# A mixer and mixture-of-experts layer on one core: pieces of 64 for heavy experts, earlier returns of weight buffers, and mask products of 128 rows

## The chip, the core and the metric

The kernel runs on one core of one Trainium2 chip. A core has four engines that compute: TensorE (PE in the profile, its weight loads PEld), VectorE (DVE), ScalarE (ACT) and GpSimd (POOL). SyncE (SP) issues DMAs; POOL and ACT can issue them too. Each engine works through its own instructions in order, and they wait for each other by semaphores. The metric is the time of one launch on the device in microseconds; lower is better.

## What is computed

One layer over 2048 tokens of width 1024. First a mixer: an RMS norm, one input projection, four heads of mLSTM and four heads of differential attention, an output projection and the residual. Then a mixture of experts, with these lines:

```python
h = rms_norm(x, norm1_w)
x = x + hybrid_mixer(h, ...)              # mLSTM heads and differential attention heads
h = rms_norm(x, norm2_w)
x = x + hierarchical_moe(h, ...)
...
# differential attention, per block of 128 queries
mask = key_chunk[None, :] <= q_chunk[:, None]          # chunks of 64 keys
p = softmax(where(mask, q @ k.T * scale, -inf))        # two maps per head
attn = p[:, :, 0] - lam * p[:, :, 1]
...
# experts: the best of 4 groups, then the best 2 of its 8 experts, for each token
weights = g_w * softmax(top_vals)
hid = silu(xb @ w_gate[e]) * (xb @ w_up[e])            # 1024 -> 512
y_expert = hid @ w_down[e]                             # 512 -> 1024
y = sum over the two experts of weights * y_expert
```

There are 32 experts and 4096 places for tokens (two for each token), 128 on average. With these inputs twelve experts get more than 128: six get 129 to 150, four get 165 to 189, two get 201 and 241.

## The kernel before

**Stages.** The input projection (to about 345 us), the heads in 64 steps (4 heads by 16 blocks of 128 queries, 345 to 1140 us), the output projection with the second norm and the choice of experts (to about 1405 us), then the experts. Weights are float32. Each is split into a high and a low part (`split_h` on ACT, line 66, `split_l` on DVE, line 70), and products are made three times (high by high, high by low, low by high).

**Mask.** In `score_atoms` two products per chunk of keys make the scores of a block (line 574). On the chunk with the diagonal, a third product (line 577) adds -1e30 where the first 64 queries meet the last 64 keys: `qm` and `km` are one row of 128 bf16 numbers each. There are 64 blocks with two maps each, so 128 such products.

**Slot tables.** `tb_d` holds for every expert a list of slots; a slot is a row of four numbers: the token to gather, half of its weight, the row to return to. Unused slots return to spare rows behind the output. `fetch_slots(i)` (line 1176) loads an expert's first 256 slots into a tile `ix2`; five such tiles exist, and the fetch for expert e+3 takes over the tile of expert e-2.

**One iteration per expert.** The first 128 slots go through TensorE with split weights: `ffn1` (line 1227, 48 products of 512 columns) for expert e, and then `ffn2` (line 1242, 24 products, called through `down(0)` to `down(3)`) for expert e-1. The result is evicted with the slot's weight (line 1247) and returned by an indirect DMA that adds into the output (`scatter`, line 1251). Every such return waits until the one before it has landed. `ready` issues the splits of the weights six halves ahead.

**Further slots.** An expert with more than 128 tokens (n > P) is heavy. Under branches on its count, `few` takes slots 129 to 160 (a piece of 32), then 161 to 192 (another piece of 32, if n > 160), then 193 to 256 (a piece of 64, if n > 192). A piece uses the raw weights in float32: its tokens are turned (line 1261), multiplied with gate and up (line 1272), turned again (line 1278) and multiplied with down (line 1287). The first piece has `down(2)` and `down(3)` of the expert before between its steps. Its result is evicted to `yE` (line 1304), scaled by the slots' weights on POOL (line 1305), and after all pieces `yE` is returned with 128 rows.

**Weights.** Twelve buffers of 1 MB hold raw weights, six for an expert. `done(e, j)` hands back buffer j of expert e, that is, SP issues the load of expert e+2 into it (lines 847 and 850, issue order on SP's queue). All six `done` of an iteration stand behind the branch: first the two `w_down` buffers of expert e-1, then the four gate and up buffers of expert e. Each DMA on SP's queue waits for the DMA eight places before it.

**Order of the experts.** A small computation on the chip ranks the experts: those over `HEAVY` = 144 tokens are spread evenly among the others, the j-th of them at (j + `LEAD`)/count. Two experts are fixed at the front. The iterations then run, with L for light, q for one piece, M for two pieces (32 + 32) and X for three: LLLLqLqqLLqLLLXLLXLLMLLLMLqMLLMq.

## Time and profile before

| | |
|---|---|
| median of 3 runs | 2278.22 us (2277.26 to 2286.74) |
| profiled execution, its own time | 2281.88 us |
| its span | 2279.8 us, 40566 instructions |
| busy: PE, PEld, DVE, ACT, POOL | 92%, 77%, 70%, 54%, 23% of the span |
| HBM over the span | 378.51 MB read, 87.65 MB written, 204 GB/s |

The span is the time from the first to the last instruction in the trace; the run's own time is 2.1 us more. The trace names each instruction by line, engine, operation and tiles, so `pgu<-H,xT` is a product that writes pgu from H and xT. Behind an instruction stand, in brackets, the idle time of its engine before it and what ended that. The DMA share is the mean busy share of the 16 DMA engines; it can pass 1 where packets overlap.

### The profile page before, as it was taken

To read this page: it belongs to the slowest core of one execution; us is meant where nothing else is said; L and a number is where in the kernel's file an instruction comes from. 1 tells how busy PE (TensorE), PEld (TensorE's weight loads), DVE (VectorE), ACT (ScalarE), POOL (GpSimd) and SP (SyncE) were. 2 spreads that over 40 slices of the span, in tenths; PEclk is the share of its full clock that TensorE was granted. 3 is DMA by queue.
4 is the path that set the end of the run, shared out by engine and by line. 5 is a ranking of instruction groups with operands and counts; after the bars stand their busy time and mean duration, and the time that the engine had idled before them with its cause. 6 is when DMAs were issued, how large, how long until landed. Compare 5 with 4: busy or idle time off the path is not lost. (4 is left out here: it accounts for less than half of the span.)

```text
span 2279.8 us, 40566 instructions
## 1 busy us (share of the span) xinstructions
PE 2099.1 (92%) x13815; PEld 1754.8 (77%) x13816; DVE 1603.2 (70%) x4373; ACT 1230.7 (54%) x2820; POOL 518.5 (23%) x684
## 2 busy tenths in 40 slices
PE   7999989999999999999999996998888999888885
PEld 6888878899999899999877884866666656665664
DVE  6667646886887687788877777876765747666562
ACT  4444324665566566566633334766665656655653
POOL 4000013223322332332111113222232222222312
PEclk9999998999999999999999997999999999999998
DMA  7656368636554663555169442999997859778783
GB/s 220 184 162 188 132 150 226 157 107 163 165 133 116 179 173 105 153 154 145 52 196 302 149 140 92 336 307 303 332 297 257 290 184 317 255 279 269 232 296 48
DMA packets 242336, 452.95 MB, mean 199 GB/s; under 512 B 36368, under 2 KB 120400, under 8 KB 232080
## 3 DMA queue, kind: packets, MB, share of 16 engines
q1 hardware_dynamic: 192160, 316.56, 41.8%
q0 software_dynamic: 49632, 131.86, 22.2%
q8 instruction: 153, 2.51, 0.5%
q10 hardware_dynamic: 272, 1.05, 0.1%
q14 instruction: 119, 0.97, 0.1%
HBM read 378.51 MB, written 87.65 MB: 204 GB/s over the span
## 5 line engine op out<-in xcount | busy, mean ns | idle before, releaser
L70 DVE TENSOR_TENSOR L<-R,H 128x1024 fp32r<-128x1024 f32 x408 | 485.4, 1221 | 184.8 <-ACT H L66 177.7
L66 ACT ACTIVATE H<-R 128x1024 fp32r<-128x1024 f32 x408 | 417.6, 1060 | 154.3 <-DMA R<-w_up 117.9
L1227 PE MATMUL pgu<-H,xT 128*128 128x512 f32 x1024 | 369.1, 418 | 49.7 <-DVE th L1209 28.7
L1227 PEld LDWEIGHTS pgu<-H,xT 128*128 128x128 f32 x1024 | 199.5, 195 | 98.5 <-ACT H L66 28.2
L589 ACT ACTIVATE prob<-sc,nm 128x512 f32<-128x512 f32 (+3 forms) x320 | 196.0, 625 | 51.0 <-DVE nm L586 45.8
L578 DVE TENSOR_REDUCE mx<-sc 128x1 f32<-128x512 f32 (+3 forms) x320 | 187.8, 605 | 35.5 <-PE sc L577 19.4
L1227 PE MATMUL pgu<-L,xT 128*128 128x512 f32 x512 | 207.6, 406 | 0.0
L574 PE MATMUL sc<-kt,qt 128*128 128x512 f32 (+3 forms) x640 | 192.7, 388 | 7.7 <-DMA kt<-k_d 7.2
L1242 PE MATMUL py<-H,hT 128*128 128x512 f32 x512 | 175.4, 405 | 2.1 <-ACT y L1247 1.1
L94 PE MATMUL w<-H,hs 128*128 128x256 f32 x512 | 156.8, 306 | 4.8 <-DVE num L694 4.8
L504 PE MATMUL w<-hs,H 128*128 128x256 f32 x512 | 159.2, 311 | 0.5 <-ACT tho L549 0.5
L633 PE MATMUL w<-va,aT 128*128 128x128 f32 x1088 | 156.3, 277 | 2.2 <-ACT raw L514 1.4
L478 POOL DMA_DIRECT2D qt<-q_d x128 | 78.1, 617 | 299.7 <-DVE g_lf L407 275.4
L633 PEld LDWEIGHTS w<-va,aT 128*128 128x128 f32 x1088 | 139.1, 191 | 8.6 <-ACT raw L514 4.1
L95 PE MATMUL w<-L,hs 128*128 128x256 f32 x512 | 145.8, 285 | 0.0
L96 PE MATMUL w<-H,hs 128*128 128x256 f32 x512 | 145.5, 284 | 0.0
L506 PE MATMUL w<-hs,L 128*128 128x256 f32 x512 | 145.4, 284 | 0.0
L505 PE MATMUL w<-hs,H 128*128 128x256 f32 x512 | 145.3, 284 | 0.0
L1242 PEld LDWEIGHTS py<-H,hT 128*128 128x128 f32 x512 | 97.5, 190 | 31.1 <-issue 7.2
L1251 POOL DMA_INDIRECT out<-y,ix x32 | 58.4, 1825 | 259.8 <-ACT y L1247 166.1
L1227 PEld LDWEIGHTS pgu<-L,xT 128*128 128x128 f32 x512 | 100.3, 196 | 19.8 <-issue 2.3
L1305 POOL TENSOR_SCALAR yE<-yE,ix 32x1024 f32<-32x1024 f32 (+1 forms) x20 | 57.0, 2848 | 253.0 <-ACT yE L1304 130.3
(373 smaller groups left out, 5283.6 us busy)
## 6 DMA issues: line engine op xcount, KB each, us to landing
R<-w_gate SPq DMA_DIRECT2D x128, 512.0 KB, 11.5
R<-w_up SPq DMA_DIRECT2D x128, 512.0 KB, 12.4
R<-w_down SPq DMA_DIRECT2D x63, 1024.0 KB, 8.2
hs<-hT_d POOLq DMA_DIRECT2D x62, 1024.0 KB, 5.4
hT_d<-hs SPq DMA_DIRECT2D x16, 1024.0 KB, 4.1
qt<-q_d POOLq DMA_DIRECT2D x128, 128.0 KB, 6.1
xt<-x SPq DMA_DIRECT2D x30, 512.0 KB, 4.4
q_d<-qkT SPq DMA_DIRECT2D x32, 256.0 KB, 3.7
```

The lines of the kernel that those rows point to most:

```text
L66: return A.activation(dst, src, AF.Copy, scale=scale)
L70: return V.tensor_tensor(dst, src, h.bitcast(F32), OP.subtract)
L94: T.matmul(ps, xh, wh, start=start, stop=False)
L95: T.matmul(ps, xh, wl, start=False, stop=False)
L96: T.matmul(ps, xl, wh, start=False, stop=stop)
L504: T.matmul(ps, l0, m0, start=d == 0, stop=False)
L574: T.matmul(ps[:, :n], QT[g // 2][:, o, m, g % 2 * P:(g % 2 + 1) * P], KT[r * 4 + c][:, m, :n], start=o == 0, stop=o == 1 and c < sb)
L578: V.reduce_max(B["mx"][:, m, c:c + 1], ps[:, :n], axis=AX.X)
L589: mark["ACT"] = A.activation(B["p", m][:, c2 * 512:c2 * 512 + n], B["sc", m, c2][:, :n], AF.Exp, bias=nm, scale=0.125, accum_out=B["rs"][: ...
L633: T.matmul(po, B["aT", c][:, kb * P:(kb + 1) * P], VA[r * 4 + c][:, kb, :], start=c == 0 and kb == 0, stop=c == nch - 1 and kb == nb[c] - 1)
L1227: T.matmul(pgu[c], xT[:, l, d, :], r[:, :, n], start=d == 0 and m == 0, stop=d == DC - 1 and m == 2)
L1242: T.matmul(py[n], hT[:, l, f, :], r[:, c], start=f == 0 and m == 0, stop=f == 3 and m == 2)
```

## The change

1. `qm` and `km` have 128 rows; all but the first are zero. The mask product runs over 128 rows and adds the same.
2. Further slots come as one piece of 32 (n up to 160) or one piece of 64 (n up to 192), and a second piece of 64 above. `few` is cut into `few_down`, `few_emit` and `few_return`.
3. The eviction of a piece takes the slot's weight as its scale. For that each table tile has three more columns of slots, laid out as the pieces lie in PSUM, and `fetch_slots` loads them with eight more small DMAs. The scaling on POOL is gone. Each piece is returned by itself, with 32 or 64 rows.
4. The `done` of the two `w_down` buffers are issued during `ffn1` (at d = 3 and 5). The `done` of the four gate and up buffers stand inside the two sides of the branch; on the light side they wait for the splits and not for the branch's end on PE.
5. `HEAVY` is 128 and `LEAD` 0.5. The order becomes LLLqLqLLqLqLLXLXLLMLqLLqLMLLMLML.
6. The tile of ones for the ranking is made later, in the pool of the output projection.

```diff
--- before.py
+++ after.py
@@ -41,8 +41,8 @@
 XAT = 1
 LOOK = 6
 PR = (0, 1, 2, 3, 4)
-LEAD = 0.7
-HEAVY = 144
+LEAD = 0.5
+HEAVY = 128
 NRM = 0.49
 QK1 = (0.0, 0.45)
 QK0 = (0.5, 0.95)
@@ -117,7 +117,6 @@
 
         ident = cp.tile([P, P], F32, name="ident")
         before = cp.tile([P, P], BF16, name="before")
-        onesb = cp.tile([P, P], BF16, name="onesb")
         nw = cp.tile([P, 2], F32, name="nw")
         cnt = cp.tile([P, NE], F32, name="cnt")
 
@@ -135,13 +134,13 @@
             V.tensor_scalar(ident, jp, 0.0, None, op0=OP.is_equal)
             V.tensor_scalar(before, jp, 0.0, None, op0=OP.is_gt)
             V.tensor_scalar(cmask, jp, 0.0, NEG, op0=OP.is_lt, op1=OP.mult)
-        V.memset(onesb, 1.0)
-        qm = c1.tile([1, P], BF16, name="qm")
+
+        qm = c1.tile([P, P], BF16, name="qm")
         V.memset(qm, 0.0)
-        V.memset(qm[:, 0:64], NEG)
-        km = c1.tile([1, P], BF16, name="km")
+        V.memset(qm[0:1, 0:64], NEG)
+        km = c1.tile([P, P], BF16, name="km")
         V.memset(km, 0.0)
-        V.memset(km[:, 64:128], 1.0)
+        V.memset(km[0:1, 64:128], 1.0)
         ones64 = c1.tile([64, P], F32, name="ones64")
         V.memset(ones64, 1.0)
 
@@ -939,6 +938,8 @@
             V.tensor_copy(m3[:, 2, :], ident[:NE, :NE])
             ones32 = sp.tile([NE, NE], F32, name="ones32", bufs=1)
             V.memset(ones32, 1.0)
+            onesb = sp.tile([P, P], BF16, name="onesb", bufs=1)
+            V.memset(onesb, 1.0)
             V.memset(cnt, 0.0)
             V.tensor_tensor(wr, wr, n2c.unsqueeze(2).to_broadcast([P, DC, NL]), OP.mult)
 
@@ -1180,9 +1181,13 @@
                     else:
                         eid[i] = nc.values_load(cnti[:1, ids_at + i:ids_at + i + 1], engines=(mybir.EngineType.SP, mybir.EngineType.Activation)[:2 if i < 3 else 1], min_val=0,
                                                 max_val=NE - 1, skip_runtime_bounds_check_because="a place's expert")
-                    IX[i] = sp.tile([P, 2, 4], F32, name="ix2", bufs=AHEAD + 2)
+
+                    IX[i] = sp.tile([P, 5, 4], F32, name="ix2", bufs=AHEAD + 2)
                     e = eid[i]
-                    nc.sync.dma_start(IX[i], tb_d[ds(e * SLOTS, 2 * P), :].rearrange("(k p) c -> p k c", p=P))
+                    nc.sync.dma_start(IX[i][:, :2], tb_d[ds(e * SLOTS, 2 * P), :].rearrange("(k p) c -> p k c", p=P))
+                    for k, m, r0 in ((2, Q, 0), (3, M, 0), (4, M, M)):
+                        for q in range(P // m):
+                            nc.sync.dma_start(IX[i][q * m:(q + 1) * m, k], tb_d[ds(e * SLOTS + P + r0, m), :])
 
             def gather(ix, xg):
 
@@ -1288,21 +1293,25 @@
                                  raw[:, q * w:(q + 1) * w], start=f == 0, stop=f == 3, skip_group_check=True)
                 return px
 
-            def few(e, m, r0, between=()):
+            def few_down(e, m, xH, between=()):
 
                 between = list(between) + [lambda: None] * 2
-                xH = few_turn_x(m, r0)
                 between[0]()
                 hH = sp.tile([P, 2, P], F32, name="hH", bufs=1)
                 th = [few_ffn1(xH, e, m, c) for c in range(m // Q)]
                 between[1]()
                 for c, t in enumerate(th):
                     few_turn_h(t, hH, c)
-                px = few_ffn2(hH, e, m)
-                w = D * m // P
+                return few_ffn2(hH, e, m)
+
+            def few_emit(e, m, r0, px):
+                w, k = D * m // P, 2 if m == Q else 3 + r0 // M
                 for q in range(P // m):
-                    A.activation(yE[r0:r0 + m, q * w:(q + 1) * w], px[q * m:(q + 1) * m, :w], AF.Copy)
-                G.tensor_scalar(yE[r0:r0 + m], yE[r0:r0 + m], IX[e][r0:r0 + m, 1, 1:2], None, op0=OP.mult)
+                    A.activation(yE[r0:r0 + m, q * w:(q + 1) * w], px[q * m:(q + 1) * m, :w], AF.Copy,
+                                 scale=IX[e][q * m:(q + 1) * m, k, 1:2])
+
+            def few_return(e, m, r0):
+                scatter(yE[r0:r0 + m], IX[e][:m, 4 if r0 else 1])
 
             engines = [mybir.EngineType.PE, mybir.EngineType.DVE, mybir.EngineType.Activation, mybir.EngineType.Pool]
             why = "counts of 2048 tokens"
@@ -1339,14 +1348,16 @@
                             turn(xTn, xg0, (d // 4,))
                             if d == 5 and e + 2 < NE:
                                 gather(IX[e + 2][:, 0], xg0)
+                        if d in (3, 5) and e:
+                            done(e - 1, 4 + d // 4)
                         if d == 4:
                             tc.mark_branch_hint_location(f"more{e}", n > P, engines)
                     thn = [hidden(p, 256) for p in pgu]
                 else:
+                    emit(*waiting)
                     hT = new_hT()
                     for d in range(2):
                         turn_h(th[d], hT, d)
-                    emit(*waiting)
                     thn = None
                 if e:
                     py = new_py()
@@ -1360,28 +1371,37 @@
                 down(0)
                 down(1)
                 if e < NE:
+                    last = (lambda: down(2), lambda: down(3))
                     with tc.If(n > P, label=f"more{e}", preferred_fallthrough_block=True) as more:
                         tc.mark_branch_hint_location(f"more{e}b", n > P + Q, engines)
-                        few(e, Q, 0, (lambda: down(2), lambda: down(3)))
-                        with tc.If(n > P + Q, label=f"more{e}b", preferred_fallthrough_block=True):
+                        with tc.If(n > P + Q, label=f"more{e}b", preferred_fallthrough_block=True) as many:
                             tc.mark_branch_hint_location(f"more{e}c", n > P + M, engines)
-                            few(e, Q, Q)
-                            with tc.If(n > P + M, label=f"more{e}c", preferred_fallthrough_block=True):
-                                few(e, M, M)
-                        scatter(yE, IX[e][:, 1])
+                            px = few_down(e, M, few_turn_x(M, 0), last)
+                            with tc.If(n > P + M, label=f"more{e}c", preferred_fallthrough_block=True) as most:
+                                xH = few_turn_x(M, M)
+                                few_emit(e, M, 0, px)
+                                few_return(e, M, 0)
+                                few_emit(e, M, M, few_down(e, M, xH))
+                                few_return(e, M, M)
+                            with most.Else():
+                                few_emit(e, M, 0, px)
+                                few_return(e, M, 0)
+                        with many.Else():
+                            few_emit(e, Q, 0, few_down(e, Q, few_turn_x(Q, 0), last))
+                            few_return(e, Q, 0)
+                        for j in range(4):
+                            done(e, j)
                     with more.Else():
-                        down(2)
-                        down(3)
+                        for f in last:
+                            f()
+                        for j in range(4):
+                            done(e, j)
                 else:
                     down(2)
                     down(3)
                 if e:
                     waiting = (py, IX[e - 1][:, 0])
-                    for j in (4, 5):
-                        done(e - 1, j)
                 if e < NE:
-                    for j in range(4):
-                        done(e, j)
                     xT, th = xTn, thn
             emit(*waiting)
             sched.__exit__(None, None, None)
```

On SP, the queue of loads, around the fetch of a later expert's table (`ix<-tb_d`) in one iteration. Before, from the fetch to the loads of `w_down`:

```order
L1185 DMA ix_18971<-tb_d 128x2x4 [waits DMASW2_49,DMASW1_49,DMASW4_49,DMASW0_49,DMAHW2_49,Activation_49,Pool_49]
L1325 TENSOR_LOAD cnti
L1363 COMPARE_AND_BRANCH
L1366 COMPARE_AND_BRANCH
L1369 COMPARE_AND_BRANCH
L1369 UNCONDITIONAL_BRANCH x2
L1366 UNCONDITIONAL_BRANCH
L1363 UNCONDITIONAL_BRANCH x2
L850 ISA
L850 DMA R_15378<-w_down 128x2x1024 [waits DMAHW3_49,DVE_49,PE_49]
L850 ISA
L850 DMA R_18092<-w_down 128x2x1024 [waits DMAHW4_49,DVE_49,PE_49]
```

After, the last four of the nine DMAs of a fetch, and what follows; the one of both halves (128x2x4) and four of 32 rows stand ahead of these rows:

```order
L1190 ISA
L1190 DMA ix_19043<-tb_d 64x4 [waits DMAHW7_49]
L1190 ISA
L1190 DMA ix_19043<-tb_d 64x4 [waits DMAHW0_49]
L1190 ISA
L1190 DMA ix_19043<-tb_d 64x4 [waits DMAHW1_49]
L1190 ISA
L1190 DMA ix_19043<-tb_d 64x4 [waits DMAHW2_49]
L1334 TENSOR_LOAD cnti
L849 ISA
L849 DMA R_15376<-w_down 128x2x1024 [waits DMAHW3_49,DVE_49,PE_49]
L849 ISA
```

The loads of `w_down` stand ahead of the branches now, and eight small DMAs stand ahead of them, each with a wait for an earlier DMA.

On PE, in the branch of a heavy expert. Before, the end of the first piece of 32 (`px<-R,hH`), the branch, and the second piece of 32 (`pt<-ident,xg` turns its tokens, `px<-R,xH` is gate and up):

```order
L1287 MATMUL px<-R_15378,hH 32x256 x8
L1287 MATMUL px<-R_18092,hH 32x256 x8
L1366 COMPARE_AND_BRANCH
L1367 REGISTER_ALU
L1434 BRANCH_PREFETCH_HINT
L1261 MATMUL pt<-ident,xg_18094 128x32 x8
L1272 MATMUL px<-R_15374,xH 32x256 x8
L1272 MATMUL px<-R_15375,xH 32x256 x8
L1272 MATMUL px<-R_15376,xH 32x256 x8
L1272 MATMUL px<-R_15377,xH 32x256 x8
L1278 MATMUL pt<-ident,th_18837 128x128
L1287 MATMUL px<-R_15378,hH 32x256 x8
```

After, behind the branch for more than 160 tokens, the piece of 64 is the first, and the products of the expert before (`py`) stand inside it:

```order
L1377 COMPARE_AND_BRANCH
L1378 REGISTER_ALU
L1454 BRANCH_PREFETCH_HINT
L1266 MATMUL pt<-ident,xg_18094 128x64 x8
L1247 MATMUL py_18704<-H_117,hT 128x512
L1247 MATMUL py_18704<-L_119,hT 128x512
L1247 MATMUL py_18704<-H_117,hT 128x512
L1247 MATMUL py_18705<-H_117,hT 128x512
L1247 MATMUL py_18705<-L_119,hT 128x512
L1247 MATMUL py_18705<-H_117,hT 128x512
L1277 MATMUL px<-R_15372,xH 64x256 x4
L1277 MATMUL px<-R_15373,xH 64x256 x4
```

The second piece of 32 is gone; the first piece has 64 rows, with `down(2)` behind its turned tokens.

On POOL, in the same branch. Before, the scalings of the three pieces and one return (`out<-yE`):

```order
L1305 ISA
L1305 TENSOR_SCALAR yE<-yE,ix_18146 32x1024 [waits Activation_49]
L1366 COMPARE_AND_BRANCH
L1367 REGISTER_ALU
L1434 BRANCH_PREFETCH_HINT
L1305 TENSOR_SCALAR yE<-yE,ix_18146 32x1024 [waits DMASW5_49,DMASW6_49,DMASW4_49,Activation_49]
L1369 COMPARE_AND_BRANCH
L1305 TENSOR_SCALAR yE<-yE,ix_18146 64x1024 [waits Activation_49]
L1369 UNCONDITIONAL_BRANCH
L1369 UNCONDITIONAL_BRANCH [waits Pool_49]
L1366 UNCONDITIONAL_BRANCH [waits Pool_49]
L1251 DMA out<-yE,ix_18146 2176x1024 [waits DMASW5_49,Activation_49,Pool_49]
```

After, returns alone, one or two for each side of the branches:

```order
L1377 COMPARE_AND_BRANCH
L1378 REGISTER_ALU
L1454 BRANCH_PREFETCH_HINT
L1380 COMPARE_AND_BRANCH
L1256 DMA out<-yE,ix_18170 2176x1024 [waits DMASW0_49,Activation_49,Pool_49]
L1256 DMA out<-yE,ix_18170 2176x1024 [waits DMAHW5_49,DMASW2_49,Activation_49]
L1380 UNCONDITIONAL_BRANCH
L1256 DMA out<-yE,ix_18170 2176x1024 [waits DMASW0_49,Activation_49,Pool_49]
L1380 ISA [waits DMASW3_49]
L1380 UNCONDITIONAL_BRANCH
L1256 DMA out<-yE,ix_18170 2176x1024 [waits DMASW0_49,Activation_49,Pool_49]
L1377 ISA [waits DMASW3_49]
```

The scalings are gone from POOL, and a return stands directly behind the branch of its piece.

## Rows read from the trace of the kernel before

**Rows 1.** Windows, attention: stretch, length, busy of PE, PEld, DVE, ACT, POOL; clock, DMA share.

```profile
440.00:540.00 100.00, 99.75 (x752) 91.40 (x751) 80.59 (x242) 63.42 (x201) 25.43 (x50) 1.00 0.44 119
```

**Rows 2.** The same view of the expert part, one stretch for one expert.

```profile
1459.40:1477.80 18.40, 18.40 (x86) 14.62 (x85) 16.80 (x20) 12.20 (x17) 6.70 (x4) 1.00 1.03 362
1602.10:1627.30 25.20, 18.49 (x86) 14.53 (x84) 14.47 (x17) 14.71 (x20) 6.45 (x5) 0.94 0.95 303
1673.60:1699.90 26.30, 18.71 (x86) 14.35 (x84) 14.12 (x17) 13.32 (x19) 7.57 (x6) 0.93 0.93 288
1906.00:1944.60 38.60, 33.91 (x294) 23.12 (x294) 23.68 (x30) 22.61 (x39) 6.42 (x3) 0.93 0.76 275
2009.10:2050.10 41.00, 33.39 (x296) 22.15 (x294) 21.29 (x27) 21.51 (x37) 5.71 (x4) 0.96 0.71 255
2165.10:2185.60 20.50, 18.32 (x85) 14.47 (x83) 13.98 (x17) 10.35 (x16) 4.36 (x3) 1.00 0.93 319
```

**Rows 3.** Timeline of PE, attention part: start, length, line, tiles, shapes; with, then without a mask.

```profile
570.27 0.63 PE L574 MATMUL sc<-kt,qt 128*128 128x512 f32 x2
570.84 0.22 PE L577 MATMUL sc<-km,qm 1*128 1x128 bf16 x1
571.21 0.28 PE L95 MATMUL w<-L,hs 128*128 128x256 f32 x1
...
388.54 0.63 PE L574 MATMUL sc<-kt,qt 128*128 128x512 f32 x2
389.12 0.28 PE L95 MATMUL w<-L,hs 128*128 128x256 f32 x1
```

**Rows 4.** Timeline of PE, output projection: two products of 128 bf16 rows.

```profile
1364.76 0.40 PE L96 MATMUL pj<-H,hs 128*128 128x512 f32 x1
1364.99 0.19 PE L1056 MATMUL prk<-ohb,before 128*128 128x32 bf16 x1
1365.37 0.49 PE L983 MATMUL pt<-ident,xt 128*128 128x128 f32 x3
```

**Rows 5.** Timelines of POOL and SP behind a heavy expert; in brackets idle time before.

```profile
1584.65 2.85 POOL L1305 TENSOR_SCALAR yE<-yE,ix 32x1024 f32<-32x1024 f32 x1 [9.22 <-ACTq L1366]
1588.45 2.13 POOL L1251 DMA_INDIRECT out<-yE,ix  x1 [0.95 <-ACT hT L66]
1599.53 1.59 POOL L1251 DMA_INDIRECT out<-y,ix  x1 [7.57 <-DMA R<-w_up]
...
1606.05 0.37 SPq L1185 DMA_DIRECT2D ix<-tb_d  x1
1607.20 1.01 SPq L850 DMA_DIRECT2D R<-w_down  x2
```

**Rows 6.** Waits of SP's queue (total, times, longest); DMA issue (median landing); expert part.

```profile
SPq L1185 <- DMA out<-y,ix: 209.1, 18, 21.5
SPq L847 <- PE py L1242: 20.2, 8, 5.3
...
out<-yE,ix POOLq DMA_INDIRECT x12, 10.1
```

**Rows 7.** Timeline of PE, the expert with 201 tokens: its three further pieces.

```profile
1736.77 0.68 PE L1261 MATMUL pt<-ident,xg 32*128 32x32 f32 x8
1747.10 0.68 PE L1261 MATMUL pt<-ident,xg 32*128 32x32 f32 x8
1756.56 0.71 PE L1261 MATMUL pt<-ident,xg 64*128 64x64 f32 x8
1758.76 7.13 PE L1272 MATMUL px<-R,xH 128*64 128x256 f32 x64 [1.48 <-ACT xH L1263]
1770.82 0.49 PE L1227 MATMUL pgu<-H,xT 128*128 128x512 f32 x1
```

**Rows 8.** Chain that ended last, in order of time: start, length, what.

```profile
2254.11 6.06 DMA out<-yE,ix
2261.07 6.46 DMA out<-y,ix
```

## Prediction

> **What bounds the kernel now.** I read the stretches first, each engine's busy time against its length. In the attention and mLSTM part (about 345 to 1140 us) TensorE is busy 99.75 of 100 us and VectorE 80.59 [rows 1]: there a nanosecond off TensorE is a nanosecond off the time, until VectorE has no room left.
>
> In the expert part (1405 us to the end) a light expert, one with at most 128 tokens, can take 18.4 us with TensorE busy all through, and the DMA share is then at 1.03 [rows 2]. So TensorE and the weight loads are both nearly full. Other light experts take 25 to 26 us and TensorE stands idle for 7 of them [rows 2]. There are six light experts with such idle time, 2.2 to 7.6 us each (first and last by size in [rows 2]), 31 us together, and all six are the second expert after a heavy one. The DMA issues say why. After a heavy expert the scaling of its rows runs on GpSimd (2.85 us), then the return of these rows goes out, and only 11 us after that the return of the previous light rows, because every return into the output waits for the one before to land (10.1 us in the middle). SyncE then fetches the next slot table, which waits for that landing (209.1 us of waiting in all, 18 times), and only behind that fetch come the weight loads [rows 5, 6]. The expert part is thus a chain return, return, fetch, weights, beside a TensorE that has little slack.
>
> **The change, part by part.**
>
> *A, mask products of 128 rows.* There are 128 (64 blocks, two maps). From the first score product to the second product behind the mask it is 570.27 to 571.21, 0.94 us; the same products without a mask take 388.54 to 389.12, 0.58 us. A mask with one row costs 0.36 us [rows 3]. What it would cost with 128 rows is bounded by two bf16 products of 128 rows and 32 columns between products of 512: 1364.76 to 1365.37 is 0.61 us, where two 512s alone take 0.46 (0.23 each), so 0.075 us each [rows 4]. With 128 columns instead of 32 I take 0.11. That leaves 0.25 us a mask, 32 us for 128; since TensorE is not alone in that part, I take −28 us. Bounds: 0 and −46 (the whole 0.36).
>
> The Trainium skill ("TensorEngine Tiling (Array Packing)", Key Properties) says that changing the tiling mode drains the engine; a one-row operand between full ones would do so twice, and the 0.36 us agrees. Against it stands "TensorE: Matmul & The Clock Gate", LDWEIGHTS: a load's time goes by columns, not rows, and so the 128-row mask would save nothing; that is a rival below.
>
> *B, one piece of 64 for two of 32.* Four experts have 165 to 189 tokens (32 + 32 before, 64 now), two have 201 and 241 (32 + 32 + 64 before, 64 + 64 now). At the expert of 201 tokens the first 32 takes 1736.77 to 1747.10, of which 12 products of the previous expert are 2.8 us (12 × 0.23), so 7.5 us; the second takes to 1756.56, 9.5 us; the 64 takes to 1770.82, 14.3 us, with 1.5 us of waiting for its turned rows [rows 7]. As first piece the 64 has these 12 products beside its waits: about 12.3 us. So 17.0 us become 12.3, and 6 × 4.7 = −28 us. The second 64 stays as it was. Bounds: with none of its waits covered the first 64 takes the whole 14.3, and the gain is 6 × 2.7 = −16; with the later start of the loads that follow counted too, −42.
>
> *C, scaling in the eviction, returns of 32 or 64 rows.* The 2.85 us on GpSimd and the 0.95 behind them go; a return of 32 rows should land nearer to the 6.06 of an idle queue than to 10.1 [rows 5, 6, 8]. The next return, and with it fetch and weights, comes some 8 us earlier, of which about 6 count, since its own rows are evicted no earlier. Twelve heavy experts; the idle time that it can take away is that of the six light experts above (31 us) and of heavy ones in the same place. I take −28 us, bounds 0 and −50.
>
> *D, eight more table DMAs in each fetch.* They stand on SyncE ahead of the weight loads. Two issues take 1.01 us with 0.37 for the second, so 0.64 from one to the next [rows 5]; eight take about 4.8 us. Each DMA on this queue also waits for the eighth before it, so that a fetch of nine lets the eight weight loads ahead of it land before anything new starts. Queued behind are w_down of the next expert and the gate and up weights of the one after it; the splits on ScalarE and VectorE wait for these, and TensorE for the splits. In a heavy expert the queue waits anyway (its DMA share is 0.71 [rows 2]), and the expert after a heavy one has its weights. In the new order 17 experts beyond the first three follow a light one: 17 × 4.8 = 82 us; part of it falls on slack, and I take +70. Bounds: 0 (all hidden) and 29 × 4.8 = +139 (every fetch on the path).
>
> The Trainium skill ("DMA: Bandwidth & Descriptors", Rules for kernel authors) says to coalesce many small transfers, since under 64 KB one pays mostly overhead; these carry 0.5 or 1 KB. No row here has nine in a row, so the size of the loss is mine.
>
> *E, order of experts.* Three experts of 129, 133 and 137 tokens now count as heavy and are spread out, and the last place goes from a 129-token to a light expert. In the end now, the heavy return (6.06 us), the return of the expert before (6.46) and the last one run one after the other [rows 8]. The first falls away: −7, and with a more even spread −10 us.
>
> *F, early hand-back.* w_down loads are issued before the branch instead of behind it, on SyncE still behind the same fetch. For light experts the loads no longer wait for TensorE to pass the branch. But SyncE comes out of the fetch so late (at 1606.05, 4 us into the next expert [rows 2, 5]) that it waited for that only 20.2 us in all, in 8 places [rows 6]. I take 0, bound −20. One more branch on some paths: 0 to +5, none taken. The memsets and the place of the ones tile: nothing.
>
> *Sum:* −28 −28 −28 +70 −10 = −24 us. Against the profiled execution's 2281.9 us this is 2258 us. The median of the runs shown, 2278.2, lies 3.7 below that execution; 0.5% of it, about what a measurement can tell, is 11.4 us.
>
> **The rivals.**
>
> *R1, the small DMAs win: slower.* Every fetch drains the weight queue, in heavy experts too, because their loads are what the next ones start from. D is then +139 and the sum +45: 2327 us. It decides against the kernel from D = +94 on. For it speaks the DMA share of 1.03 in light experts; against it that SyncE idles for long in heavy ones.
>
> *R2, the masks save nothing.* If only the 128 columns count, A is 0: 2286 us. The skill's LDWEIGHTS rule would give this. Against it speak 0.36 us beside 0.075 us for products that differ in rows [rows 3, 4].
>
> *R3, the small DMAs are hidden.* SyncE has several us free in each expert, and D is +20: 2208 us. Against it: these free us lie ahead of the fetch, not behind it.
>
> *R4, the earlier returns bring nothing,* because the fetch then waits for the queue's own eight loads instead of the landing: C is 0, 2286 us.
>
> **How the numbers follow.** Forecast 2258 with 0.50 (its own range 2240 to 2276), R1 0.15, R2 0.13, R3 0.12, R4 0.10. The range 2215 to 2300 holds the forecast, R2 and R4 and the nearer part of R1 and R3, about 0.82. Faster by over 0.5% (under 2266.8): most of the forecast and R3, 0.60. Within: R2, R4 and the forecast's upper edge, 0.23. Slower: R1 and a little more, 0.17.
>
> **What would show it.** A: a stretch with mask at about 0.69 us instead of 0.94, and the attention part 25 us or more shorter; 0.94 would be R2. B: an expert of 178 to 189 tokens at some 34 us instead of the 38.6 and 41.0 of [rows 2], with one piece of 64. C: the light return within 8 us of the start of an expert that follows a heavy one. D: weight loads some 5 us behind the fetch instead of 1, and more idle time before the first product of experts that follow a light one; if the light ones run at 18.4 throughout, it is R3, and if heavy ones stall at their start as well, R1. E: no heavy return in the last chain. The prediction is wrong as a whole if the expert part gets longer by more than the attention part gets shorter.

## The result and the profile after

The change makes the kernel slower: 2302.2 us (median of 6 runs, 2294.3 to 2308.8) against 2280.3 of before (6 runs), a ratio of 1.0092 (95%: 1.0066 to 1.0117). The forecast was 2258. The profiled execution of after took 2302.95 us.

The front part got shorter as meant: the first product of the experts starts at 1386.3 instead of 1405.1 us. From there to the end it takes 914.8 us instead of 874.7. So 19 us are won in front, and 40 lost where the forecast had 4 us more.

The windows of after (columns as in [rows 1] and [rows 2]): the attention part, then five experts, which are a light one right behind a heavy one, a light one that is the second behind a heavy one, and heavy ones of 150, 189 and 178 tokens.

```profile
440.00:540.00 100.00, 98.90 (x770) 92.36 (x769) 82.10 (x250) 63.11 (x200) 28.79 (x54) 1.00 0.48 128
...
1474.90:1493.10 18.20, 18.20 (x89) 14.72 (x86) 14.39 (x18) 17.75 (x25) 7.53 (x5) 1.00 1.00 330
1548.30:1574.00 25.70, 18.30 (x85) 14.46 (x83) 14.83 (x18) 11.87 (x17) 4.91 (x3) 0.90 0.77 254
1574.00:1611.00 37.00, 30.17 (x190) 20.70 (x190) 23.11 (x28) 18.44 (x27) 2.95 (x2) 0.79 0.78 269
1881.80:1924.90 43.10, 35.25 (x174) 23.16 (x175) 23.72 (x30) 20.79 (x32) 3.52 (x2) 0.87 0.72 247
2076.60:2119.60 43.00, 33.02 (x176) 21.91 (x174) 21.22 (x27) 17.08 (x27) 3.92 (x2) 0.88 0.66 225
```

The light expert right behind a heavy one is as good as before. The second one still loses 7 us, and the heavy experts, which follow a light one in this order, now idle too: 6.8 to 10 us each, at a granted clock of 0.79 to 0.88. The two of 189 and 178 tokens run the one piece of 64 and yet take 43 us, where before took 38.6 and 41.0 [rows 2].

The waits of the expert part (total, times, longest) tell where the idle time lies. First TensorE's two largest in after, then ScalarE's largest; behind them the same three in e2, a run below that has one of the eight small DMAs.

```profile
PE px L1277 <- ACT xH L1268: 64.0, 13, 8.3
PE pgu L1232 <- DVE th L1214: 40.8, 6, 10.1
ACT H L66 <- DMA R<-w_up: 173.8, 49, 13.4
```
```profile
PE px L1275 <- ACT xH L1266: 9.6, 5, 3.6
PE pgu L1230 <- DVE th L1212: 5.3, 2, 3.2
ACT H L66 <- DMA R<-w_up: 77.4, 37, 7.5
```

So the larger part is not at the start of an expert but inside the heavy ones, at the first product of the further slots (`px`). The timelines of ScalarE and TensorE in the 150-token expert:

```profile
1595.29 2.00 ACT L66 ACTIVATE H<-R 128x1024 fp32r<-128x1024 f32 x2 [8.38 <-DMA R<-w_up]
1600.19 0.42 ACT L1268 ACTIVATE xH<-pt 128x128 f32<-128x128 f32 x2
1600.50 6.54 PE L1277 MATMUL px<-R,xH 128*32 128x256 f32 x64 [6.43 <-ACT xH L1268]
```

ScalarE waits 8.4 us for weights that it is to split (`H<-R`). The eviction of the turned tokens (`xH`) needs no load, but stands behind these splits in ScalarE's order, and TensorE waits 6.4 us for it. Eleven of the twelve heavy experts have such a wait, of 2.9 to 8.3 us, each behind a split that waited 5.8 to 11.6 us for `w_up`.

SyncE's timeline of after (start, length, line, tiles, count) tells why the weights come late, beside [rows 5]:

```profile
1513.84 0.43 SPq L1187 DMA_DIRECT2D ix<-tb_d  x1
1515.08 9.90 SPq L1190 DMA_DIRECT2D ix<-tb_d  x8
1525.56 1.07 SPq L849 DMA_DIRECT2D R<-w_down  x2
```

From the start of the main fetch to that of the first weight load it is 11.7 us. The 28 fetches of the expert part have a mean of 9.4 us (5.8 to 12.2), where before it was 1.5 (28 fetches, 1.1 to 5.5). The waits of SyncE's queue in the expert part of after (total, times, longest) name what the eight small DMAs stand for, beside [rows 6]:

```profile
SPq L1187 <- DMA out<-y,ix: 152.9, 14, 20.8
SPq L1190 <- DMA R<-w_up: 48.2, 62, 1.6
SPq L1190 <- DMA R<-w_gate: 35.6, 49, 1.4
```

111 times a small DMA waits for a weight load to land. In the DMA packets of after the weight queue stands still for 3.3 us at nearly every fetch besides its longer pauses: 34 pauses over 0.5 us, 218 us together, against 18 pauses and 165 us before.

### The profile page after: what moved, and what is told of

Its sections match the earlier page's. It is cut to its first block, busy times and chain, and to the rows that moved or that the text cites. A ratio compares the mean times of both kernels' runs of the same rounds, so it can differ in the third digit from the quotient of the medians.

```text
span 2301.1 us, 39633 instructions
## 1 busy us (share of the span) xinstructions
PE 2082.0 (90%) x13095; PEld 1745.5 (76%) x13096; DVE 1600.7 (70%) x4373; ACT 1217.9 (53%) x2772; POOL 465.0 (20%) x666
## 5 line engine op out<-in xcount | busy, mean ns | idle before, releaser
L1232 PE MATMUL pgu<-H,xT 128*128 128x512 f32 x1024 | 368.6, 418 | 53.4 <-DVE th L1214 40.8
L1277 PE MATMUL px<-R,xH 128*64 128x256 f32 (+1 forms) x896 | 103.7, 480 | 66.2 <-ACT xH L1268 64.0
L1277 PEld LDWEIGHTS px<-R,xH 128*64 128x64 f32 (+1 forms) x896 | 57.6, 156 | 112.1 <-ACT xH L1268 69.9
L1194 POOL DMA_INDIRECT xg<-h_d,ix x64 | 92.8, 1449 | 127.7 <-PE pt L1205 53.3
```

The lines of the kernel that those rows point to most:

```text
L1232: T.matmul(pgu[c], xT[:, l, d, :], r[:, :, n], start=d == 0 and m == 0, stop=d == DC - 1 and m == 2)
L1277: T.matmul(px[q * m:(q + 1) * m, :2 * P], xH[:, d, :m], w[:, :, h * P:(h + 1) * P], start=d == 0, stop=d == DC - 1, skip_group_check=True)
```

## The experiments

Theory T1: the eight table DMAs of a fetch run the weight queue dry, and that is where the time went. Rivals: T2, the order and the place of the branch; T3, SyncE's time for the DMAs alone. Each ratio is against the kernel before, run beside it on the same chip, where it took 2280 to 2289 us; the 95% interval stands in brackets.

**e1 and e2: three table DMAs a fetch, and one.**

```diff
-                        for q in range(P // m):
-                            nc.sync.dma_start(IX[i][q * m:(q + 1) * m, k], tb_d[ds(e * SLOTS + P + r0, m), :])
+                        rows = tb_d[ds(e * SLOTS + P + r0, m), :]
+                        nc.sync.dma_start(IX[i][:, k], rows.unsqueeze(0).to_broadcast([P // m, m, 4]))
```

> The changed kernel with its eight extra table DMAs per fetch made three (one for each slot, the four copies of 32 rows and the two of 64 rows read by one DMA each through a repeated source); everything else as changed. Theory T1: the eight of them wait, one after the other, for the weight loads eight places ahead on SP to land, so the weight queue runs dry at every fetch, and that is what the expert part lost; three of them reach back only to the second half of the eight loads of gate and up, so the queue keeps work. Then the expert part goes from 915 us to 825 to 850 and the time from 2302 to 2212 to 2237. Rival T2: the table DMAs are beside the point, and the heavy experts lose their time at their start through the order of the experts and the later hand-back (a branch that now ends with its own loads): 2295 to 2305.

```diff
-                    for k, m, r0 in ((2, Q, 0), (3, M, 0), (4, M, M)):
-                        for q in range(P // m):
-                            nc.sync.dma_start(IX[i][q * m:(q + 1) * m, k], tb_d[ds(e * SLOTS + P + r0, m), :])
+                    nc.sync.dma_start(IX[i][:M, 4], tb_d[ds(e * SLOTS + P + M, M), :])
...
-                                 scale=IX[e][q * m:(q + 1) * m, k, 1:2])
+                                 scale=IX[e][q * m:(q + 1) * m, 1, 1:2])
```

e2 leaves out the right weights: without the seven DMAs its evictions scale by those of other tokens, so its output is not the layer's, while number, place and size of the work stay.

> The changed kernel with one extra table DMA per fetch, that of the rows from 192 up, whose indices the second piece of 64 needs; the scaled evictions read the weights of the wrong tokens from the second group of rows on, which leaves their number, place and size as they are. T1: as with three, or up to 15 us less, 2197 to 2230, and the first weight load starts within 2 us of the main fetch. T2: 2295 to 2305. A third view, T3, that it is the number of SP's instructions (some 0.6 us each) and not the waits: about 17 x 7 x 0.6 = 70 us less than 2302 here and 50 less with three, so 20 us between the two runs.

Three: 2254.5 us, ratio 0.9855 (0.9823 to 0.9887). One: 2205.2, ratio 0.9648 (0.9611 to 0.9684). So seven of the eight DMAs cost 97 us (101 by the ratios), and T2 falls: order, branch and pieces are the same in all three. But three DMAs cost more than T1 gave them: T3's price puts e1 at 2252, near what it took, but e2 at 2232, 27 us too long. SyncE's timeline of e1:

```profile
1507.03 0.37 SPq L1187 DMA_DIRECT2D ix<-tb_d  x1
1507.61 6.74 SPq L1190 DMA_DIRECT2D ix<-tb_d  x3
1515.45 1.05 SPq L849 DMA_DIRECT2D R<-w_down  x2
```

Here the wait for a landing is short, but the issue of the third DMA itself takes 3.67 of the 6.74 us; 22 of the 96 issues took over 1 us. When the next weight load is issued, hardly anything is left in the queue: by the DMA packets it moved 1.53 MB of weights from 1510 to 1514 us and 0.50 MB from 1514 to 1518. The Trainium skill ("DMA: Bandwidth & Descriptors", Rules for kernel authors) says to coalesce small transfers; the trace agrees, with 48 us for the same bytes in three DMAs instead of eight, and shows that it is not enough.

In e2 these places are shorter again: the second light expert behind a heavy one runs at 18.1 us, and the heavy ones of 150, 189 and 178 tokens (windows, columns as above) at 30.0, 34.6 and 37.2.

```profile
1540.50:1558.60 18.10, 18.10 (x86) 14.65 (x85) 15.39 (x19) 10.30 (x15) 4.89 (x3) 1.00 0.94 314
1558.60:1588.60 30.00, 26.58 (x191) 18.96 (x189) 22.65 (x26) 20.05 (x28) 3.66 (x2) 0.94 1.05 374
1831.60:1866.20 34.60, 32.93 (x175) 22.47 (x175) 23.67 (x30) 20.24 (x31) 2.86 (x2) 0.92 0.87 304
2000.20:2037.40 37.20, 31.91 (x176) 21.36 (x174) 21.37 (x27) 17.07 (x27) 3.92 (x2) 0.95 0.76 258
```

**e3: the eight DMAs on the kernel before** (the tile of ones is made later, as in the change).

```diff
+                    ixs = sp.tile([P, 3, 4], F32, name="ix3", bufs=AHEAD + 2)
+                    for k, m, r0 in ((0, Q, 0), (1, M, 0), (2, M, M)):
+                        for q in range(P // m):
+                            nc.sync.dma_start(ixs[q * m:(q + 1) * m, k], tb_d[ds(e * SLOTS + P + r0, m), :])
```

> The kernel before with the eight table DMAs of the change added to each fetch, into a tile that nothing reads; the pieces, returns, masks and order stay as before. T1: the expert part goes from 875 us to 950 to 985, the time to 2355 to 2390 (rival R1 of the prediction put the price at up to +139, its sum at +70: 2351). T2, and rival R3 of the prediction: the DMAs are hidden, 2275 to 2286.

2394.2 us, ratio 1.0463 (1.0428 to 1.0498): +107 us, a little over T1's upper end. The 32 experts up to TensorE's last instruction, in one window each of before, e3, after and e2:

```profile
1405.10:2262.00 856.90, 754.25 (x4751) 557.56 (x4750) 559.90 (x678) 527.92 (x793) 218.82 (x125) 0.96 0.81 268
```
```profile
1406.60:2376.50 969.90, 778.35 (x4751) 569.56 (x4750) 560.31 (x678) 528.92 (x792) 218.90 (x126) 0.91 0.73 238
```
```profile
1386.30:2288.60 902.30, 764.58 (x4031) 560.66 (x4030) 560.72 (x679) 518.08 (x744) 167.63 (x108) 0.92 0.76 252
```
```profile
1389.60:2191.90 802.30, 742.60 (x4031) 552.81 (x4030) 561.02 (x678) 518.71 (x744) 170.46 (x107) 0.97 0.85 283
```

The same 4751 products take 24.1 us longer in e3 than before, beside 89 us more of idle time, and the mean granted clock goes from 0.96 to 0.91. After and e2 have the same 4031 products: 100 us apart, 78 of idle time and 22.0 in the products themselves (0.92 and 0.97). The DMAs' price thus has two parts, the stall and the slower products behind it.

TensorE's timeline at the start of the 150-token expert, in after and in e2, shows the second part:

```profile
1574.03 0.76 PE L1232 MATMUL pgu<-H,xT 128*128 128x512 f32 x1 [7.43 <-DVE th L1214]
1574.59 0.63 PE L1232 MATMUL pgu<-L,xT 128*128 128x512 f32 x1
```
```profile
1558.79 0.40 PE L1230 MATMUL pgu<-L,xT 128*128 128x512 f32 x1
```

After 7.4 us of standing still the same product takes 0.63 instead of 0.40 us, until about 1579: the granted clock is 0.50 (1.2 of 2.4 GHz) from 1574 to 1579 us and 1.00 from 1579.2 to 1585. The Trainium skill ("TensorE: Matmul & The Clock Gate", HAM oscillation) says that after such a wait for data the next products start at the lower clock; the trace agrees, with a granted clock of 0.79 over this expert and 0.94 in e2.

**e9: the eight DMAs behind the weight loads instead of ahead of them.**

```diff
-                    for k, m, r0 in ((2, Q, 0), (3, M, 0), (4, M, M)):
...
                         for j in range(4):
                             done(e, j)
+                        fetch_more(e + AHEAD)
```

> The changed kernel with its eight table DMAs moved behind the eight gate and up loads of the same turn instead of ahead of the two w_down loads; number and size unchanged. T1, that their wait for the DMA eight places ahead runs the queue dry: it does so here too, since the eight reach back to exactly the eight loads, 2270 to 2300. T3, that it is SP's time ahead of the loads (7.7 us between a main fetch and the first load behind it that were not there before): that time now lies where SP has nothing to issue, 2205 to 2230.

2250.6 us, ratio 0.985 (0.9821 to 0.9879), between the two. SyncE's timeline:

```profile
1527.56 14.42 SPq L1193 DMA_DIRECT2D ix<-tb_d  x8
1542.85 0.40 SPq L1187 DMA_DIRECT2D ix<-tb_d  x1
1543.85 1.03 SPq L849 DMA_DIRECT2D R<-w_down  x2
```

The first load now follows the main fetch by 1.0 us, so T3's cost is gone. But the eight sit for 14.4 us until the eight loads ahead have landed, and the weight queue still stands still for 3.6 us or more at nearly every fetch. So 52 us of the change's 2302 are won back by the place alone, and 45 above e2 remain. That the 45 are the DMAs' wait for the loads and the 52 SyncE's time ahead of them is argued from the timelines, not shown by a run. Neither T1 (2270 to 2300) nor T3 (2205 to 2230) alone gives the time.

**e4: only the masks of 128 rows, on the kernel before.** The edit is that of the change at `qm` and `km`.

> The kernel before with nothing but the mask products of 128 rows. The prediction's step A: 28 us less, 2252, if all that a mask saves comes through. From the traces: 0.227 us a mask on TensorE, 29 us in all, but TensorE's idle time between masks rose and the first expert product came 18.8 us earlier only: 2259 to 2267. Rival R2 (a mask saves nothing): 2278 to 2283.

2273.3 us, ratio 0.9934 (0.9908 to 0.9961): 9 to 21 us less. R2 falls, 28 is too much, and the 13 to 21 us less that the traces of after had suggested agree. The window of e4 that answers to [rows 1]:

```profile
440.00:540.00 100.00, 98.89 (x771) 92.38 (x770) 82.31 (x246) 62.80 (x197) 27.73 (x53) 1.00 0.47 124
```

More products fit into the 100 us (771 instead of 752), and TensorE now idles for 1.1 of them instead of 0.25.

**e5: no table DMAs.** The weights are multiplied in on GpSimd again; the two experts over 192 tokens hand back once.

```diff
-                                 scale=IX[e][q * m:(q + 1) * m, k, 1:2])
+                G.tensor_scalar(yE[r0:r0 + m], yE[r0:r0 + m], IX[e][r0:r0 + m, 1, 1:2], None, op0=OP.mult)
...
-                                few_return(e, M, 0)
                                 few_emit(e, M, M, few_down(e, M, xH))
-                                few_return(e, M, M)
+                                few_return(e, P)
```

> The changed kernel without any of the eight table DMAs: pieces of 64, 128-row masks, early returns of the rows in use and the order of the experts stay; the weights of a heavy expert's rows are multiplied in on POOL as before (2.85 us for 128 rows), and the two experts with more than 192 tokens hand back all 128 rows at once. The output is the whole one. T1 (the table DMAs alone cost the gain): 2195 to 2212, as with one of them (2205) less what that one cost, plus 3 us of POOL ahead of each of 14 returns, of which little is on the path. Rival (scaling in the eviction is what brings the return forward): 2215 to 2235.

2226.3 us, ratio 0.9714 (0.9689 to 0.9739). This version, which beats before and after, lies 21 us above e2: the rival's range, so that scaling in the eviction seems worth something. It is the base of e6, e7, e8 and e10.

**e6: e5 in the old order** (`LEAD = 0.7`, `HEAVY = 144`).

> As the kernel without table DMAs, but with the old order of the experts (a lead of 0.7, and heavy from 145 tokens). Step E of the prediction: the new order is worth 10 us, so 10 us more than the kernel of this call with the new order. Rival: with the returns early no order puts a wait in the last chain, 0 to 3 us more.

2219.0, ratio 0.9692 (0.9665 to 0.9718): 7 us less than e5, within the error, and no 10 us more.

**e7: e5 with all 128 rows handed back** (`few_return(e, P)` everywhere).

> As the kernel without table DMAs, but every heavy expert hands back all 128 rows of its second piece, as before. Step C of the prediction took 28 us for scaling in the eviction and short returns together; the scaling is already undone, the rows are the larger part: 12 to 28 us more. Rival R4 of the prediction (earlier returns bring nothing): 0 to 4 us more.

2242.1, ratio 0.9788 (0.9758 to 0.9818): 16 us more. The heavy return lands in 8.4 us in the middle instead of 6.6, and the light return behind it (behind the 145-token expert) goes out 14.1 us after the start of the next expert instead of 12.9 (in e2 10.1). R4 falls.

**e8: e5 with two pieces of 32 for one of 64.**

```diff
-                            px = few_down(e, M, few_turn_x(M, 0), last)
+                            few_emit(e, Q, 0, few_down(e, Q, few_turn_x(Q, 0), last))
+                            few_emit(e, Q, Q, few_down(e, Q, few_turn_x(Q, Q)))
...
```

> As the kernel without table DMAs, but the slots from 128 to 191 as two pieces of 32, as before. Step B: six experts need the second 32, 4.7 us each, 28 us more (bounds 16 and 42). Rival: TensorE is not what bounds a heavy expert, whose weight loads take 18 us and whose own chain waits for evictions: under 10 us more.

2280.3, ratio 0.9964 (0.9945 to 0.9984): 54 us more, above the bound of 42. The 189-token expert takes 44.6 us instead of 34.7 in e5. TensorE's timeline of its end in e8, with its second piece of 32, and two windows of the same stretch:

```profile
1887.10 0.68 PE L1263 MATMUL pt<-ident,xg 32*128 32x32 f32 x8
1889.18 3.66 PE L1274 MATMUL px<-R,xH 128*32 128x256 f32 x64 [1.40 <-ACT xH L1265]
1894.70 1.93 PE L1289 MATMUL px<-R,hH 128*32 128x256 f32 x32 [0.43 <-ACT hH L1281]
1901.21 0.77 PE L1229 MATMUL pgu<-H,xT 128*128 128x512 f32 x1 [4.57 <-ACT H L66]
```
```profile
1886.00:1892.00 6.00, 4.60 (x84) 2.71 (x80) 0.00 (x0) 1.95 (x6) 2.86 (x1) 1.00 0.00 1
1892.00:1901.20 9.20, 3.08 (x49) 1.36 (x42) 1.51 (x3) 3.11 (x7) 2.84 (x1) 0.88 0.35 117
```

The second piece takes 9.5 us, and it reads the raw weights. While it does, nothing is loaded (DMA share 0.00): SyncE issues the next load of a gate at 1896.79, when the piece is through. The next expert's first product then waits 4.57 us for weights, where in e5 it waits 1.42. So here the piece costs its own time and the stall of the next expert.

**e16: one piece of 64 alone, on the kernel before.** The edit is that of the change in the branch, with `few` as it was.

> The kernel before with one piece of 64 in place of two of 32, for the six experts with over 160 tokens; POOL still scales and all 128 rows go back at once. Step B of the prediction: 28 us less (16 to 42), 2258. If the size found by undoing it (54 us) doesn't hang on the rest: 2225 to 2240. A piece's own time from the traces is 4 us an expert, 24 in all; anything over that is weight loads that are freed earlier and the clock after a shorter stall.

2248.3, ratio 0.9828 (0.9795 to 0.9861): 40 us less, between the forecast and e8. So the piece is worth 40 to 54 us. By the traces the six experts themselves are 24 us shorter in e16 than before, 4 each, and 44 us longer in e8 than in e5; the rest falls on other experts.

**e10: e5 with the six loads issued behind the branch again.**

> The kernel without table DMAs (2226), with the issue of the six loads put back behind the branch. Step F of the prediction: 0 to 20 us more, taken 0; 2226 to 2246. Rival (it is the early hand-back that leaves light experts at 18.2 us): over 20 us more.

2222.4, ratio 0.9723 (0.9698 to 0.9748): no difference from e5 that can be measured.

**e15: the change in the old order.**

> The changed kernel with nothing but the old order (a lead of 0.7, heavy from 145 tokens). Step E of the prediction: 10 us longer than the change, 2312. If the sign found without the table DMAs holds here as well: 2285 to 2297. If the eight table DMAs, which make every heavy expert wait at its start, cover the order's effect: 2298 to 2306.

2310.2, ratio 1.0097 (1.0064 to 1.0129), beside the change's 1.0092: the order does nothing that can be measured beside the eight DMAs.

**e11 to e14: the weights by TensorE,** in both orders, without a table DMA and with one.

```diff
+                for q in range(P // m):
+                    T.matmul(pt[q * m:(q + 1) * m, 0, 0:1], ident[:, r0:r0 + m], IX[e][:, 1, 1:2], start=True, stop=True)
+                wS = sp.tile([P, 1], F32, name="wS", bufs=2)
+                V.tensor_copy(wS, pt[:, 0, 0:1])
...
```

> No table DMAs, and the weights of a piece's rows brought to its groups of rows by two or four one-column TensorE products with slices of the identity into a bank that is free, copied by VectorE, so that the eviction can scale as in the change and POOL need not. The output is the whole one. If the 21 us between the run with one table DMA (2205) and that with none (2226) are POOL's 2.85 us ahead of each return: 2203 to 2212. If they are something else: 2222 to 2232.

> The same with the old order (a lead of 0.7, heavy from 145 tokens). With POOL scaling the old order was 7 us shorter, within the error of the two; step E of the prediction held the new one 10 us shorter. If the order's worth depends on the light returns at the heavy experts' heels, it gains nothing here: 0 to 8 us less than with the new order, 2196 to 2210; by step E 2213 to 2222.

> The kernel with the weights brought by TensorE (2221), with one table DMA per fetch added again, for the indices of the rows from 192 up, so that the two experts with more than 192 tokens hand back in two parts as in the change. If the early return of these two made the run with one table DMA shorter: 2203 to 2212. If it was that run's eviction scale, which needs nothing from TensorE and VectorE: 2219 to 2232, as one DMA costs 0 to 10 us.

> The same in the old order of the experts. By the two pairs so far the old order is 7 to 15 us shorter: 2190 to 2205 or 2206 to 2225, after which of the two the run before it meets.

e11: 2221.1 (0.9707, 0.9681 to 0.9733). e12: 2206.4 (0.9651, 0.963 to 0.9673). e13: 2223.6 (0.973, 0.9695 to 0.9765). e14: 2220.0 (0.9708, 0.9669 to 0.9748). One table DMA and the early return of the two largest experts, added together, change nothing that can be measured (e13, e11). So e2's lead of 21 us over e5 (15 by the ratios) isn't theirs. Of it these products win back 5 us at most, within the error (e11, e5). The waits of TensorE in e11 show one that is not in e2:

```profile
PE pt L1234 <- DVE L L70: 28.5, 18, 4.0
```

e12 is the fastest version with the whole output: 80 us less than before.

**e17 and e18: the same products in a bank that is in use anyway.**

```diff
+                if c == 0:
+                    for q in range(P // m):
+                        T.matmul(pt[q * m:(q + 1) * m, 1, 0:1], ident[:, r0:r0 + m], IX[e][:, 1, 1:2], start=True, stop=True)
...
```

> As the kernel with the weights brought by TensorE and no table DMA (2221), but the one-column products go into the bank that the transposes of the hidden rows use anyway, instead of one more turn of the two transpose banks. In that kernel TensorE waited 18 times, 28.5 us in all, at the first transpose of the hidden rows for a VectorE split of weights, a wait that the runs without the extra turn don't have. If the extra turn made it (every later user of the pair meets the other bank, in light experts too): these waits are gone and the time is 2195 to 2208. If the waits come from the products or VectorE's copies themselves: 2216 to 2226.

> The same in the old order of the experts. The old order was 7 to 15 us shorter without table DMAs in two pairs and 4 us shorter, within the error, with one: 2185 to 2203 if it is shorter in itself, as long as the run before it (plus or minus 5) if not.

2244.6 (0.981, 0.9781 to 0.9839) and 2230.4 (0.9749, 0.9715 to 0.9782): worse. The wait stays:

```profile
PE pt L1234 <- DVE L L70: 31.1, 18, 5.2
```

So the extra turn of the banks did not make it. That VectorE's copy does is argued only (it is what both versions add to VectorE in the branch). Of the 23 us between e17 and e11 the trace names some 8: TensorE waits 11.4 us for `hH`, the turned hidden rows, in e17, where in e5 it waits 3.7. The rest stays open, and with it what of e2's 21 us is the eviction's scale.

## Why the prediction was wrong, step by step

The expert part got 40 us longer and the front 19 us shorter, the prediction's own sign of being wrong as a whole. It missed by 46 us (+22 instead of −24). By the terms measured below D is 27 to 37 of them, A 13 and E 10, while B was better by 12.

**D, the eight table DMAs: the step that failed.** The forecast took +70; the runs show +97 (after less e2) and +107 (e3). Its count was right: comparing after with e2 expert by expert, 16 experts take over 2 us longer, all of them among the 17 that follow a light one, and the experts behind a heavy one pay nothing. The price of a place was wrong. The sum had 4.8 us for it, from issue times, and took 12 us off the total for slack. Measured are 78 us of idle time, 4.9 a place, and 22 us in which the products behind the stalls run at the lower clock, 1.4 a place, a term that the sum did not have. That 4.9 meets 4.8 is luck: SyncE issues the first load 7.9 us later in a fetch than before, some of which is covered, and the idle time added in a place goes from 0.5 to 10 us.

The path was wrong in part as well. The prediction looked for the idle time before the first product of an expert. There TensorE's waits grew by 35 us (5.3 to 40.8), but at the first product of the further slots by 54 (9.6 to 64.0), through ScalarE's order: late weights hold up splits, and these the eviction of `xH`. Whether the eviction ahead of the splits would save that was not run.

**R1** has the outcome, not the count. Every fetch holds the loads up, and the heavy experts stall, though mostly not at their start. But its +139 counted 29 fetches; the experts behind a heavy one run at 18.2 us and pay nothing, as D had it. D passed the +94 from which R1 decides, and the kernel is slower. What spoke against R1, that SyncE idles in heavy experts, was true of SyncE but not of the weights: the heavy experts follow light ones, and in the one followed here, that of 150 tokens, the late loads stand behind a fetch issued in the light one ahead (at 1568.28 us).

**R3** falls by e3, **R2** by e4, **R4** by e7.

**A: mis-sized, −15 (9 to 21) instead of −28.** TensorE's part was about right: from the last score product to the second product behind the mask the median of the 128 masks fell from 0.64 to 0.42 us, 0.22 each, 28 us for all, against 0.25 forecast. In [rows 3] the first product behind the mask is left out; it is the first row here, with the rows of after below. It started 0.15 us behind the start of the mask and now starts 0.04 behind it; the second started 0.37 behind and now starts 0.24 behind.

```profile
570.99 0.39 PE L94 MATMUL w<-H,hs 128*128 128x256 f32 x1
```
```profile
568.29 0.71 PE L573 MATMUL sc<-kt,qt 128*128 128x512 f32 x2
568.85 0.23 PE L576 MATMUL sc<-km,qm 128*128 128x128 bf16 x1
568.89 0.37 PE L94 MATMUL w<-H,hs 128*128 128x256 f32 x1
569.09 0.28 PE L95 MATMUL w<-L,hs 128*128 128x256 f32 x1
```

But TensorE stands still more, and the discount from 32 to 28 was too small for that: from the first to the last mask its busy time is 23.5 us shorter, its idle time goes from 8.0 to 18.5, and the stretch is 13 us shorter, not 25. The one-row operand between full ones does cost time, as the Trainium skill ("TensorEngine Tiling (Array Packing)", Key Properties) let expect: in the median the mask starts 0.17 us behind the last score product instead of 0.26, and the next product 0.04 us behind it instead of 0.15. That this is a drain of the engine no run shows. The rule of the Trainium skill that a load goes by columns ("TensorE: Matmul & The Clock Gate", LDWEIGHTS) holds in the traces too: the load takes 0.091 us with one row and 0.096 with 128. R2 was wrong to take it for the whole cost.

**B: right in sign, too small.** −40 alone (e16), within its bounds of −16 and −42, and −54 with the rest (e8). The two experts that it named take 34.6 and 37.2 us in e2, near the 34 forecast. What the sum left out, and held only in its bound of −42, is that a shorter heavy expert gives its weight buffers back earlier, so that the next stalls less; e8 shows this at the expert behind that of 189 tokens.

**C: about right, −28 forecast.** The short return is 16 us (e7). For the eviction's scale the runs give between 5, within the error (e11 against e5), and 21 (e2 against e5), so 21 to 37 together. In after the light return goes out 10.6 us after the start (1530.1 us) of the expert behind a heavy one, where 8 was forecast and before had 15.7. On GpSimd, beside [rows 5], the heavy return and the light one:

```profile
1533.09 1.35 POOL L1256 DMA_INDIRECT out<-yE,ix  x1 [28.10 <-ACT yE L1310]
...
1540.69 1.79 POOL L1256 DMA_INDIRECT out<-y,ix  x1 [4.79 <-ACT H L66]
```

SyncE's wait for it fell from 209.1 [rows 6] to 152.9 us, but its waits of the small DMAs for weight loads, 83.8 us, stand beside it.

**E: wrong, 0 instead of −10.** The heavy return is gone from the last chain as foreseen (one return of 5.98 us stands there in place of the two of [rows 8]), but the order costs elsewhere: in all four pairs without the eight DMAs or with one the old order was the shorter, by 7 (e5, e6), 15 (e11, e12), 4 (e13, e14) and 14 us (e17, e18), two of them well within the error, and beside the eight it makes no difference (e15). Three more experts count as heavy and get a place behind a light one; where that costs was not traced.

```profile
2282.66 5.98 DMA out<-y,ix
```

**F: right,** 0 (e10, without the table DMAs).

The terms measured singly, −15, −40, −29 (the middle of C), 0 and +107, sum to +23 us; after less before is +22. The ranges of A, B and C are wide enough that so close a sum is partly luck.

## What to carry to other kernels

A DMA of 0.5 KB costs what it keeps waiting, not what it moves: on a queue where each DMA waits for the eighth before it, count how many loads may still be under way when the next one is issued, and keep small DMAs out of it, first by doing without them and then by merging. Whether another engine's queue would carry them for less was not run. Look also for what stands behind a late load in the order of the engine that waits for it. Price a stall of TensorE with the slower products behind it, and price a shorter use of a buffer with the stall that it spares the next user. When a part of a change is priced by a count times a duration, let the discount for slack be argued by a row, or leave it out.

## What the runs showed of the hardware that was not expected

- A DMA issue can itself take long when many loads are still under way: 3.67 us for a table DMA in e1, with a wait for a landing ahead of it of only 0.6 us. In the trace of before 3 of 155 issues took over 1 us where at most 2.5 MB of loads had not landed, and 30 of 77 (up to 5.5 us) where it was 4 MB or more; a free issue takes 0.37 us.
- Behind a stall the granted clock stays low for several us. In e8 TensorE stands still for 4.9 us, and the 18 products of the next 6 us run at a mean clock of 0.55, near 1.2 of 2.4 GHz (windows of e8). Over the experts of after, with 78 us more idle time than in e2, the same 4031 products took 22 us longer.

```profile
2128.80:2136.00 7.20, 2.31 (x9) 1.56 (x10) 3.55 (x5) 3.64 (x4) 0.00 (x0) 0.90 1.06 388
2136.00:2142.00 6.00, 6.00 (x18) 4.66 (x18) 5.88 (x7) 5.34 (x9) 0.11 (x1) 0.55 1.03 395
```

- Seven DMAs of 0.5 or 1 KB cost about 3 us of the kernel's time per fetch (97 us over 32 fetches); in e3, where nothing reads them, eight cost 107.
